# SSD mixer with y kept channels first, group roots through GpSimd's queue, and the convolutions dealt out one per weight piece

## The chip, the cores and the metric

The kernel runs on one core of one Trainium2 chip. The metric is the device time of the whole program in microseconds. TensorE is called PE here, its weight loads PEld, VectorE DVE, ScalarE ACT, GpSimd POOL, SyncE SP.

## The reference

A two-layer decoder trunk over 256 tokens of width 2048. Layer 0 is a Mamba-2 mixer, layer 1 an attention over keys and values made from layer 0's output. The change lies in layer 0, which computes, cut to what matters:

```
def _ssd_mixer(h, in_w, conv_w, conv_b, dt_bias, A_log, D_skip, norm_g, out_w):
    z, xBC, dt = jnp.split(h @ in_w, [4096, 4096 + 6144], axis=-1)
    xBC = jax.nn.silu(_causal_depthwise_conv(xBC, conv_w, conv_b))
    xs, Bm, Cm = jnp.split(xBC, [4096, 5120], axis=-1)        # 64 heads of 64; 8 groups of 128
    dt = jax.nn.softplus(dt + dt_bias); A = -jnp.exp(A_log)
    y = _ssd_chunked(xs * dt[..., None], dt * A, Bm, Cm)      # one chunk of 256 tokens
    y = y + (xs * D_skip[:, None]).reshape(bsz, L, 4096)
    y = y * jax.nn.silu(z)
    yg = y.reshape(bsz, L, 8, 512)
    yg = yg * lax.rsqrt(jnp.mean(jnp.square(yg), -1, keepdims=True) + RMS_EPS)
    return (yg.reshape(bsz, L, 4096) * norm_g) @ out_w
```

With one chunk and no state before it, y of a group is (C B^T, times the decays of its eight heads, causal) times the dt-scaled x. All is float32. A product with a weight is made of three matmuls: a value a is split into a high half that the fast form holds exactly and the low rest, and hi·hi, hi·lo and lo·hi are summed.

## The kernel before

**Weights.** Every weight comes in pieces of 128 x 1024 floats (512 KB), loaded by `load_piece` through SP's queue into `raw` (six buffers). `split` (lines 97 to 103) makes the halves: ACT copies the high half `whi` (line 100), DVE subtracts to the low half `wlo` (line 102); there are four buffers of each.

**Two forms of product.** In `cm_piece` (lines 141 to 153) the weight stands in the array and the activations move, 256 columns (all tokens) at a time; the output has channels on partitions. A piece is 24 matmuls. In `tm_piece` (lines 213 to 235) the activations stand and the weight moves, 512 columns at a time; the output has tokens on partitions. A piece is 12 matmuls. `cm_quad` and `tm_chunk` run the pieces of one output of 512 channels; `cm_wide` is a third form for 256 channels with both halves of the activations moving together.

**Order.** The opening (to about 175 us) makes h from the condition vector column by column on DVE (line 317) and already runs pieces of several products, in an order written out by hand (lines 540 to 552); partial sums are put away in tiles that are free by then (`begun`, lines 378 to 381). In that order stand 27 pieces of z products. Then a loop over the eight groups of the SSD follows (lines 835 to 849). In one round: the B and C product (every second round), the scores of group g, the x product of group g+1, the root scaling of group g-1 (`stage3`), the decays of group g and its x turned to tokens first (`stage1`), the four convolutions of group g+1 one after the other, the z product of group g+1, the head products of group g (`stage2`). The last z product carries group 7's scores and the first y tiles (`last_product`).

z, and with it y, have tokens on partitions: `stage2` multiplies the masked scores (standing, 64 columns at a time) with 64 channels, the sum of squares comes out of ACT's square (`accum_out`, line 812), the root scales rows on ACT (`stage3`), and `y_tiles` (lines 857 to 869) turns y back to channels first by 64 transposes on PE, scales it by the norm weight and splits it into halves for the out projection.

**Out projection.** Four chunks of 512 outputs with 16 pieces each (lines 942 to 965). Chunk 0 turns the y of one more group before every second piece (`y_ahead`). `background` takes jobs from a list at a fixed rate: these are the remaining columns of the condition product, each 1 MB from HBM and one DVE instruction of 128 x 2048 (line 317), and `gate_out`, which turns the finished gate into a row, writes it to HBM, and from there it is broadcast.

**What sets the order on an engine.** The text above is traced, and a planner orders each engine's queue when the whole program is traced, by the order of the text among what it reckons to be ready; `tc.issue_after` pins one instruction behind another. Each engine's queue, SP's and POOL's DMA queues too, then runs in that order. POOL does nothing before the last 15 us.

## Time and profile before

| | |
|---|---|
| median of three runs | 1224.19 us (1223.19 to 1224.21) |
| the profiled execution | 1223.81 us, its span 1222.0 |
| granted clock | 0.999 |
| PE, DVE, ACT, POOL busy | 99%, 83%, 58%, 0% |
| HBM read | 331.45 MB, 274 GB/s over the span |

A line of a group reads: line, engine, operation, output and inputs, shapes, count, then busy time and mean duration, then the idle time of the engine before them and what ended it. Records of matmuls overlap, so their mean duration is longer than the distance between them; the pace is read from start times. A line of the timeline or the chain begins with its start and length in us.

### The profile page before, as it was taken

Reading aid. Unit: us, or ns where it says so; the run is one execution under the profiler, and the core shown is the slowest. Engines: PE = TensorE matmul, PEld = TensorE weight load, DVE = VectorE, ACT = ScalarE, POOL = GpSimd, SP = SyncE. Lnnn points to the kernel's source line nnn. Section 1 sums busy time; section 2 is a strip of 40 time slices with the busy share of each in tenths; the row PEclk is TensorE's granted clock in tenths of the full one; section 3 lists DMA queues with packets and bytes.
Section 4 is the critical chain, followed back from the end, with each engine's and each line's share of the span. In section 5 each row is a group of like instructions: output and inputs, shape, how many; then the busy total and the mean of one; then the engine's idle time right before and its main releaser. Section 6 shows DMA issues by size and latency. Waiting matters only on the chain.

```text
span 1222.0 us, 19072 instructions
## 1 busy us (share of the span) xinstructions
PE 1208.8 (99%) x7244; PEld 1039.5 (85%) x7244; DVE 1019.6 (83%) x1450; ACT 703.9 (58%) x1057; POOL 3.9 (0%) x8
## 2 busy tenths in 40 slices
PE   8999999999999999999999999999999999999998
PEld 8889998898888888788888888888888888888886
DVE  6989997899988999899778588888987885756886
ACT  4554567787698898764335455444435844444751
POOL 0000000000000000000000000000000000000001
PEclk9999999999999999999999999999999999999999
DMA  9999976796765556689998668989997875365673
GB/s 374 421 421 423 422 264 239 259 327 224 230 190 194 182 173 207 226 327 334 370 317 298 211 203 342 350 344 379 385 376 280 281 261 174 113 193 160 193 260 69
DMA packets 81372, 335.94 MB, mean 275 GB/s; under 512 B 9200, under 2 KB 9984, under 8 KB 68480
## 3 DMA queue, kind: packets, MB, share of 16 engines
q1 hardware_dynamic: 80496, 333.59, 75.6%
q0 software_dynamic: 576, 1.05, 0.6%
q8 instruction: 57, 0.93, 0.3%
q14 instruction: 35, 0.29, 0.1%
q10 hardware_dynamic: 208, 0.08, 0.0%
HBM read 331.45 MB, written 3.23 MB: 274 GB/s over the span
## 4 chain that ended last, share of the span: by engine, by line
PE 77%; DVE 13%; ACT 5%; DMA 3%; issue 2%; DVEq 0%; ACTq 0%
PE acc L224 25%; PE acc L190 21%; PE acc L193 11%; DVE wlo L102 4%; DVE araw L317 4%; PE acc L233 3%; PE acc L234 3%; PE acc L232 3%; DMA raw<-in_win 3%; ACT whi L100 2%; DVE cacc L391 2%; PE acc L151 1%; PE acc L153 1%; PE acc L152 1%; PE py L809 1%
## 5 line engine op out<-in xcount | busy, mean ns | idle before, releaser
L100 ACT ACTIVATE whi<-raw 128x1024 fp32r<-128x1024 f32 x389 | 408.2, 1057 | 329.5 <-PE acc L190 107.1
L102 DVE TENSOR_TENSOR wlo<-raw,whi 128x1024 fp32r<-128x1024 f32 x389 | 470.2, 1221 | 128.3 <-ACT whi L100 121.1
L190 PE MATMUL acc<-actT,whi 128*128 128x512 f32 x1280 | 401.7, 394 | 0.5 <-DVE xs L202 0.5
L193 PEld LDWEIGHTS acc<-actT,wlo 128*128 128x128 f32 x1280 | 239.6, 188 | 52.3 <-DVE wlo L102 0.7
L193 PE MATMUL acc<-actT,wlo 128*128 128x256 f32 x1280 | 255.2, 281 | 0.3 <-DVE wlo L102 0.3
L317 DVE SCALAR_TENSOR_TENSOR araw<-araw,cb__72 128x2048 f32<-128x2048 f32 x95 | 217.0, 2284 | 3.2 <-DMA araw<-in_ada 3.0
L190 PEld LDWEIGHTS acc<-actT,whi 128*128 128x128 f32 x1280 | 195.0, 188 | 1.7 <-DVE xs L202 0.9
L224 PE MATMUL acc<-whi,actT 128*128 128x512 f32 x560 | 144.5, 392 | 0.5 <-ACT whi L100 0.5
L224 PEld LDWEIGHTS acc<-whi,actT 128*128 128x128 f32 x560 | 104.2, 188 | 22.0 <-ACT whi L100 0.9
L233 PE MATMUL acc<-wlo,actT 128*128 128x512 f32 x272 | 106.8, 393 | 2.2 <-DVE wlo L102 2.1
L232 PE MATMUL acc<-whi,actT 128*128 128x512 f32 x272 | 105.0, 394 | 0.2 <-ACT sz L664 0.2
L151 PE MATMUL acc<-actT,whi 128*128 128x256 f32 x372 | 103.5, 281 | 1.0 <-ACT sz L664 0.5
L224 PE MATMUL acc<-wlo,actT 128*128 128x512 f32 x384 | 103.6, 391 | 0.0
L153 PE MATMUL acc<-actT,wlo 128*128 128x256 f32 x372 | 101.9, 281 | 1.5 <-DVE wlo L102 1.5
L152 PE MATMUL acc<-actT,whi 128*128 128x256 f32 x372 | 103.0, 279 | 0.0
L234 PE MATMUL acc<-whi,actT 128*128 128x512 f32 x256 | 100.0, 391 | 0.0
L224 PEld LDWEIGHTS acc<-wlo,actT 128*128 128x128 f32 x384 | 71.7, 188 | 14.4
L151 PEld LDWEIGHTS acc<-actT,whi 128*128 128x128 f32 x372 | 69.6, 188 | 2.6 <-ACT sz L664 0.9
L153 PEld LDWEIGHTS acc<-actT,wlo 128*128 128x128 f32 x372 | 68.9, 188 | 2.3 <-DVE wlo L102 2.3
L152 PEld LDWEIGHTS acc<-actT,whi 128*128 128x128 f32 x372 | 70.6, 190 | 0.2
L233 PEld LDWEIGHTS acc<-wlo,actT 128*128 128x128 f32 x272 | 51.1, 188 | 13.8 <-DVE wlo L102 3.7
L232 PEld LDWEIGHTS acc<-whi,actT 128*128 128x128 f32 x272 | 50.9, 188 | 10.5 <-ACT sz L664 0.6
(324 smaller groups left out, 1293.5 us busy)
## 6 DMA issues: line engine op xcount, KB each, us to landing
araw<-in_ada SPq DMA_DIRECT2D x96, 1024.0 KB, 7.3
raw<-in_win SPq DMA_DIRECT2D x109, 512.0 KB, 6.0
raw<-in_wout SPq DMA_DIRECT2D x64, 512.0 KB, 5.7
raw<-in_wbin SPq DMA_DIRECT2D x64, 512.0 KB, 4.1
raw<-in_wxs SPq DMA_DIRECT2D x48, 512.0 KB, 4.5
raw<-in_wv SPq DMA_DIRECT2D x48, 512.0 KB, 6.7
raw<-in_wk SPq DMA_DIRECT2D x48, 512.0 KB, 7.6
cbc<-cumd SPq DMA_DIRECT2D x16, 512.0 KB, 5.1
```

What stands on the lines that cost most here:

```text
L100: copied.append(S.activation(hi, raw, AF.Copy))
L102: latest.append(V.tensor_tensor(lo, raw, hi.bitcast(F32), op=ALU.subtract))
L151: T.matmul(o, hi[:, k, c_], ahi[:, kt, :], start=first, stop=False, skip_group_check=True)
L152: T.matmul(o, hi[:, k, c_], alo[:, kt, :], start=False, stop=False, skip_group_check=True)
L153: T.matmul(o, lo[:, k, c_], ahi[:, kt, :], start=False, stop=kt == k1 - 1, skip_group_check=True)
L190: T.matmul(ps[n], hi[:, k, n * P:n * P + P], both(kt), start=kt == 0, stop=False, skip_group_check=True)
L193: T.matmul(ps[n][:, 0, :], lo[:, k, n * P:n * P + P], high(kt), start=False, stop=kt == KT - 1, skip_group_check=True)
L224: T.matmul(ps[b], a_(kt)[:, b * P:b * P + P], w_[:, k, :], start=a_ is ahi and w_ is hi and kt == k0, stop=w_ is lo and kt == k1 - 1)
L232: T.matmul(o, h_, hi[:, k, :], start=kt == k0, stop=False, skip_group_check=part)
L233: T.matmul(o, h_, lo[:, k, :], start=False, stop=False, skip_group_check=part)
L234: end = T.matmul(o, l_, hi[:, k, :], start=False, stop=kt == k1 - 1, skip_group_check=part)
L317: return V.scalar_tensor_tensor(raw, raw, 1.0, cb_, op0=ALU.mult, op1=ALU.mult, accum_out=mod[layer][:, ct, j:j + 1])
```

## The change

What changes, part by part:

- z is computed with `cm_quad`, so with channels on partitions, in the opening and in the loop; `tm_chunk` serves only the out projection and layer 1.
- y of a group is a tile of 128 x 4 x 256 (channels in four tiles, tokens along the row). The head products have x (64 channels) standing and 128 tokens of masked scores moving; the state product is four matmuls of 128 columns. The decay factors of the second half of the tokens are exponentials of the broadcast sums (`grow`), made on ACT. The D term is four scaled copies on ACT in place of two DVE multiplications.
- The sum of squares goes over partitions: one square on ACT into z's tile, two sums on DVE, two matmuls of one column against ones. The root goes to HBM (`rootd`) through POOL's DMA queue and comes back as a broadcast to all partitions, again through POOL: singly for groups 0, 1, 6 and 7, in one for groups 2 to 5. DVE scales y by norm weight and root in one step per channel tile (`y_scale`), and `y_split` makes the halves: one instruction of 1024 columns on ACT and one on DVE.
- The four convolutions of an x group become `chores`: one is taken after each weight piece of the following products; what is left is done before the next `stage1`, and in round 6 at once.
- In the out projection chunks 0 and 1 run their first 14 pieces each, then the last two of chunk 0 and of chunk 1, which hold group 7. Group 7's sums and root are traced in front of piece 1 of chunk 0, its tiles in front of piece 2 of chunk 1. Background jobs come once in three pieces there (before: one in two in chunk 0 and one in four later), then two in five.
- The second stage's matmuls are pinned behind the last product in groups 0, 2, 3, 4 and 7 (before: 0, 4 and 7), and one behind another.

The diff, cut:

```diff
-    def cm_quad(src, ahi, alo, rate=(0, 1), k0=0):
+    def cm_quad(src, ahi, alo, rate=(0, 1), k0=0, pre=None):
         ps = acc_pair()
         for q in range(k0 // 2, KT // 2):
+            if pre:
+                pre(q)
...
             background(*rate)
+            if chores:
+                chores.pop(0)()
+        z_end[:] = [end]
         return ps
...
+                return [lambda n=n: conv(t[:, n, :], 4 * g + n, t[:, n, :]) for n in range(4)]
...
+                ps = cm_quad(src, hhi, hlo, rate=R, k0=k0, pre=pre)
                 if kind == "z":
-                    ps = tm_chunk(src, hh_, hl_, rate=R, k0=k0, pre=pre, low_last=False)
...
+                    for n, rows_ in enumerate((slice(0, 64), slice(64, 128))):
+                        S.activation(grow[rows_, 2 * w:2 * w + 2, :], cbc[rows_, n:4:2, 1, :], AF.Exp)
...
+                for i in range(4):
+                    S.activation(y[g][:, i, :], xs[g][:, i, :], AF.Copy, scale=pv("dsk")[:, 4 * g + i:4 * g + i + 1])
+                return segs, xd, cb, xo, grow
...
+                behind = z_end[-1] if g in (0,2,3,4,7) else None
+                for i in range(4):
+                    c_ = slice(i * P, i * P + P)
+                    with tc.issue_after(behind.ins) if behind is not None else ExitStack():
+                        behind = T.matmul(po[:, c_], xo[:, c_], cb[:, 2, :], start=True, stop=True)
+                xo = xo.rearrange("p (i n) -> p i n", i=4)
+                V.tensor_tensor(xo, po.rearrange("p (i n) -> p i n", i=4), grow, op=ALU.mult)
+                V.tensor_tensor(y[g][:, :, P:], xo, y[g][:, :, P:], op=ALU.add)
+                for w in range(2):
+                    py = aux2.tile([P, 2, L], F32, name="py")
+                    for b in range(2):
+                        for hh in range(4):
+                            h = 4 * w + hh
+                            t_ = slice(64 * (hh % 2), 64 * (hh % 2) + 64)
+                            with tc.issue_after(behind.ins):
+                                behind = T.matmul(py[t_, hh // 2, b * P:b * P + P], xd[:, b, 64 * h:64 * h + 64],
+                                         segs[w][:, hh, b, :], start=True, stop=True)
+                    c_ = slice(2 * w, 2 * w + 2)
+                    V.tensor_tensor(y[g][:, c_, :], py, y[g][:, c_, :], op=ALU.add)
+                V.tensor_tensor(y[g], y[g], sz[g], op=ALU.mult)
+                sq = sz[g]
+                S.activation(sq, y[g], AF.Square)
+                return sq
+
+            def stage3(g, sq):
+
+                V.tensor_tensor(sq[:, 0:2, :], sq[:, 0:2, :], sq[:, 2:4, :], op=ALU.add)
+                sums = sq[:, 0, :]
+                V.tensor_tensor(sums, sums, sq[:, 1, :], op=ALU.add)
+                ss = (aux if g == G - 1 else aux2).tile([P, 512], F32, name="aux" if g == G - 1 else "py")[:, :2]
                 for b in range(2):
+                    T.matmul(ss[:, b:b + 1], sums[:, b * P:b * P + P], ones[:, 0:1], start=True, stop=True)
                 ms = sm.tile([P, 2], F32, name="ms")
                 V.tensor_scalar(ms, ss, 1.0 / 512, EPS, op0=ALU.mult, op1=ALU.add)
+                nc.gpsimd.dma_start(rootd[g * L:g * L + L].rearrange("(b p) -> p b", p=P), rsqrt(ms, "a"))
...
-                convolve = product("xs", g + 1)
+                convs = product("xs", g + 1)
+                while chores:
+                    chores.pop(0)()
                 if rs is not None:
                     stage3(g - 1, rs)
                 st1 = stage1(g, cb)
-                convolve()
+                chores.extend(convs)
+                while chores and g == G - 2:
+                    chores.pop(0)()
...
+            def y_scale(g):
+
+                if g < 2:
+                    roots[g] = p0.tile([P, L], F32, name="cacc", bufs=3)
+                    bcast(roots[g], rootd, g * L, queue=PO)
+                elif g in (2, 6):
+                    t = slots.tile([P, 4, L], F32, name=f"s{g // 6}")
+                    roots.update({g + j: t[:, j, :] for j in range(min(4, G - g))})
+                    n = min(4, G - 1 - g)
+                    bcast(t[:, :n, :].rearrange("p i l -> p (i l)"), rootd, g * L, queue=PO)
+                elif g == G - 1:
+                    bcast(roots[g], rootd, g * L, queue=PO)
+                for i in range(4):
+                    V.scalar_tensor_tensor(y[g][:, i, :], y[g][:, i, :], pv("normg")[:, 4 * g + i:4 * g + i + 1],
+                                           roots[g], op0=ALU.mult, op1=ALU.mult)
+
+            def y_split(g):
+
+                val = y[g].rearrange("p i (j r) -> p i r j", r=2)
+                hi, lo = (t.rearrange("p i (r j) -> p i r j", r=2) for t in y_to(g))
+                S.activation(hi, val, AF.Copy)
+                V.tensor_tensor(lo, val, hi.bitcast(F32), op=ALU.subtract)
...
         def y_ahead(q):
+            if q == 1:
+                with tc.high_priority():
+                    stage3(G - 1, rs)
+            if q % 2 == 0 and q // 2 + 1 < G - 1:
                 y_tiles(q // 2 + 1)
...
+        def out_pieces(n, q0, q1, pre=None):
+            for q in range(q0, q1):
+                if pre:
+                    pre(q)
+                tm_piece(wout[n], q, pss[n], out_of(0), out_of(1), 0, 2 * KT, low_last=True)
+                background(1, 3)
+
+        out_pieces(0, 0, KT - 2, y_ahead)
+        out_pieces(1, 0, KT - 2, lambda q: y_tiles(G - 1) if q == 2 else None)
+        drain()
...
+        for n in range(2):
+            out_pieces(n, KT - 2, KT)
+            joined(n, pss[n])
+        for n in range(2, 4):
+            ps = tm_chunk(wout[n], out_of(0), out_of(1), nk=2 * KT, rate=(2, 5), pre={3: first_weights}.get(n),
+                          split_end=4 if n == 3 else 0)
```

168 lines of the change are left out of this document (63 added, 105 removed).

## The prediction

> **What bounds the kernel now.** I read the page first, then the windows by stage, the waits, the pace of matmuls in the timeline, and last the two places where VectorE (DVE) sets the pace.
>
> ```profile
> span 1222.0 us, 19072 instructions
> PE 1208.8 (99%) x7244; PEld 1039.5 (85%) x7244; DVE 1019.6 (83%) x1450; ACT 703.9 (58%) x1057; POOL 3.9 (0%) x8
> PE 77%; DVE 13%; ACT 5%; DMA 3%; issue 2%; DVEq 0%; ACTq 0%
> ```
>
> The profiled run took 1223.81 us, 1.8 more than its span, and 0.4 less than the median of the three timed runs (1224.19). PE is busy for 99%, but overlapped records hide a PE that is paced by others. So the windows and the waits:
>
> ```profile
> 126.00:142.00 16.00, 16.00 (x134) 15.81 (x133) 15.44 (x18) 5.58 (x7) 0.00 (x0) 1.00 1.02 422
> 454.00:482.00 28.00, 28.00 (x253) 24.35 (x250) 26.44 (x50) 24.97 (x48) 0.00 (x0) 1.00 0.65 214
> 482.00:511.00 29.00, 28.30 (x196) 22.88 (x192) 25.57 (x50) 23.10 (x43) 0.00 (x0) 1.00 0.47 164
> 511.00:562.00 51.00, 51.00 (x252) 41.46 (x252) 49.40 (x77) 30.47 (x50) 0.00 (x0) 1.00 0.85 314
> PE acc L233 <- DVE wlo L102: 2.1, 3, 1.0
> ```
>
> The columns are stretch, length, busy time of PE, PEld, DVE, ACT and POOL, granted clock, DMA share, GB/s. PE is full in the opening (first row), in the SSD loop (454 to 482) and at the start of the out projection (511 to 562), while DVE stands at 94 to 97% beside it in all three. Only the last z product (482 to 511) leaves DVE 3.4 us. PE's longest wait in all is 2.1 us, on the low half of a weight. So the time is PE's queue: a matmul taken away is gained, one added is lost, and DVE has next to nothing to spare where the change gives it work.
>
> The pace of the two forms of product:
>
> ```profile
> 561.67 119.72 PE acc L224 x528
> 143.00 0.28 PE L152 MATMUL acc<-actT,whi 128*128 128x256 f32 x1
> 143.47 0.28 PE L153 MATMUL acc<-actT,wlo 128*128 128x256 f32 x1
> 210.11 0.28 PE L152 MATMUL acc<-actT,whi 128*128 128x256 f32 x1
> 211.92 0.28 PE L153 MATMUL acc<-actT,wlo 128*128 128x256 f32 x1
> ```
>
> A matmul of 512 columns takes 119.72/528 = 0.2267 us, a piece of 12 then 2.72 us. Of 256 columns, the five matmuls from 143.00 to 143.47 (in the opening) stand 0.1175 us apart, the seventeen from 210.11 to 211.92 (a bc product of the loop) 0.113.
>
> **1. The y transposes go (-8.2).** With y kept channels first, the 64 transposes of y_tiles vanish.
>
> ```profile
> L864 PE MATMUL aux<-cc,s 128*128 128x128 f32 x64 | 11.8, 274 | 0.0
> 510.83 0.66 PE L864 MATMUL aux<-cc,s 128*128 128x128 f32 x4
> 511.25 2.09 PE L224 MATMUL acc<-whi,xs 128*128 128x512 f32 x8
> 530.03 0.38 PE L864 MATMUL aux<-cc,s 128*128 128x128 f32 x2
> 530.16 0.48 PE L224 MATMUL acc<-whi,actT 128*128 128x512 f32 x1
> 530.48 0.38 PE L864 MATMUL aux<-cc,s 128*128 128x128 f32 x2
> ```
>
> Four in a row hold PE for 0.42 us (510.83 to 511.25). A pair costs 0.13, and the matmul behind it 0.32 in place of 0.227: coming back to the weights costs 0.09 each time. Over the whole chunk n=0, from 511.25 to 561.67, 16 pieces of 2.72 would be 43.5 us and 50.4 passed, so the transposes in it were worth 6.9. The eight of group 0 in the last z product add 2 x 0.42 + 4 x 0.09 = 1.2, and a bit over. I take 8.2; bounds 7.5 and 9.
>
> **2. The state and head matmuls (-1.4), and the sums (+2.8).**
>
> ```profile
> 240.75 1.02 PE L798 MATMUL aux<-xo,cb 128*128 128x512 f32 x2
> 241.70 2.08 PE L809 MATMUL py<-xd,seg 128*64 128x64 f32 x64
> 243.71 0.38 PE L151 MATMUL acc<-actT,whi 128*128 128x256 f32 x1
> ```
>
> The head products take 2.01 us per group now: 64 instructions of 64 columns, 0.031 each, since the two halves of the array run side by side (a lone 128-column one takes 0.105, above; 64 would take half). Afterwards they are 32 of 128 columns, again alternating halves: 32 x 0.105/2 + some 0.15 = 1.83, so -0.18 per group, -1.4 for eight. Were the halves not side by side, it would be 32 x 0.105 = 3.4, +11 in all: the far bound. The state product (0.95) becomes four products of 128 columns, eight instructions of 0.105: even. New are two matmuls of one column per group (four instructions) that sum the squares over partitions. No row shows one column; between 0.031 (64 columns) and 0.105 (128 with a full weight), nearer the middle as the weight is full, 4 x 0.065 + 0.09 for coming back = 0.35, times 8 = +2.8; bounds 1.7 and 4.1.
>
> **3. z turned round (+2.8).** All 64 z pieces go from 12 matmuls of 512 to 24 of 256. In the order of the opening stand 27 z pieces, 37 follow in the loop. In the loop 24 x 0.113 = 2.72, even. In the opening the nearest row is 0.1175 for the same form in the same stretch: 27 x 24 x 0.0042 = +2.7, with rounding 2.8. If the slower pace belongs to those products and not to the stretch, it is 0: bounds 0 and 2.8. What could hide it is a wait of PE there, and the first window has none. A rule to weigh: the Trainium skill (TensorE: Matmul & The Clock Gate, "Back-to-back issue gap") gives a warm gap of columns over the clock plus about 2.5 ns for each matmul. By it the 768 added matmuls cost an estimated 1.9 us anywhere; the loop's 0.113 against half of 0.2267 shows no such cost, the opening shows more, so I keep the rows.
>
> **4. Start of the out projection (+2.2).** DVE sets the pace there already:
>
> ```profile
> 515.84 0.16 DVE L814 TENSOR_SCALAR ms<-ss 128x2 f32<-128x2 f32 x1
> 525.26 0.15 DVE L281 SCALAR_TENSOR_TENSOR ay<-at,ay 128x2 f32<-128x2 f32 x1
> 544.45 2.28 DVE L317 SCALAR_TENSOR_TENSOR araw<-araw,cb__72 128x2048 f32<-128x2048 f32 x1
> 546.66 0.87 DVE L869 SCALAR_TENSOR_TENSOR ylo<-aux,prm,actT 128x256 fp32r<-128x256 f32 x2
> 547.45 2.35 DVE L102 TENSOR_TENSOR wlo<-raw,whi 128x1024 fp32r<-128x1024 f32 x2
> 550.84 2.28 DVE L317 SCALAR_TENSOR_TENSOR araw<-araw,cb__72 128x2048 f32<-128x2048 f32 x1
> ```
>
> A round of two pieces lasts 6.39 us (544.45 to 550.84): two weight splits 2.27, a gate column 2.21, four L869 at 0.40. Afterwards PE wants 2 x 2.72 = 5.44 per round. DVE has two splits 2.27, four scalings by root and norm weight 1.6 (like L869), one low half of 1024 columns 1.14 (like a split), and at one column in three pieces 1.47: 6.48. Five rounds (groups 2 to 6) are 5.2 short; the first round carries group 7's tail (about 5.5: state multiply and add, two head adds, the gate multiply, two sums, the root) and comes out 4.9 short. Against that stand three pieces split ahead (3.4) and PE's own 3.0 on group 7's matmuls: 3.7 short, of which the fourth column (2.2) may trail: 1.5 to 3.7, I take 2.2. The idle 3.4 before 511 is no help: the scalings of groups 0 and 1 and the low half of group 0 (3.2 + 1.1 for 1.6 now) take 2.7 of it. Lower bound 0: group 7's tail is wanted only 28 pieces later and may run behind the rest. The second chunk stands beside it with DVE work of 1.14 + 0.74 per piece, so nothing builds up. Group 7, moved behind 28 pieces, is off the path: 76 us cover its chain. The gate row must now arrive within about five pieces (13.6 us) of its column:
>
> ```profile
> s<-gated SPq DMA_DIRECT2D x3, 256.0 KB, 8.6
> gated<-row SPq DMA_DIRECT2D x2, 8.0 KB, 2.5
> out<-u POOLq DMA_DIRECT2D x4, 256.0 KB, 8.1
> cbc<-cumd SPq DMA_DIRECT2D x16, 512.0 KB, 5.1
> ```
>
> 2.5 + 8.6 + about 1 for the transpose and copy is 12.1: hidden by 1.5; without that cover the third chunk starts late by as much as the rest, up to 3 us if loads ahead on SP hold it.
>
> **5. The loop (-1.5).** The largest PE wait there follows a burst:
>
> ```profile
> 228.72 2.76 DVE cacc L391 x7
> 231.47 1.14 DVE wlo L102
> 232.66 0.50 PE acc L233
> ```
>
> Seven convolution steps run before the split that PE stands for. One convolution behind each weight piece breaks such runs; of the 2.1 us I take 1.5. DVE per group: the two multiplications by D go (0.68 each), two sums of 512 and 256 columns come (0.68 + 0.42), so -0.3.
>
> ```profile
> L781 DVE TENSOR_TENSOR s<-aux,prm 128x512 f32<-128x512 f32 x16 | 10.9, 680 | 0.0
> L820 ACT ACTIVATE s<-s,ay 128x512 f32<-128x512 f32 x16 | 10.9, 715 | 2.0 <-DVE ay L281 2.0
> L868 ACT ACTIVATE actT<-aux,prm 128x256 fp32r<-128x256 f32 x28 | 12.3, 468 | 9.0 <-PE aux L864 9.0
> ```
>
> ACT per group loses two copies (1.4) and wins four multiplications by D and four exponentials of 256 columns, like L868 at about 0.4: 3.2. That is +1.8, less 0.3 for one square in place of two. In 454 to 482 it idles 3.0, so it lies beside. Bounds -2.1 to +4 (ACT late).
>
> **Sum:** -8.2 - 1.4 + 2.8 + 2.8 + 2.2 - 1.5 = -3.3 on 1223.8: 1220.5, on the scale of the median **1220.9**.
>
> **Rivals.**
> *More gain:* DVE keeps up at 511 (group 7's tail runs late) and the opening costs nothing: -3.3 - 2.2 - 2.8 = -8.3, 1215.9. For it: loop pace 0.113. Against: DVE's 97%.
> *Roots late (the slow side):* POOL's queue holds the write of group 7's root and the broadcast of roots 2 to 5, traced in that order. If they run so, the broadcast waits for the root, now ready at 525.4, 14.2 after the chunk's start, later by the sums (1.3); write and broadcast then take 1.3 + 6.6 (between the 5.1 of SP's broadcast and POOL's 8.1): 23.4, and 2.7 of scaling and split follow, where piece 4 wants group 2 at 10.9. PE stands about 15: -3.3 + 15 = +11.7, 1235.9; half of it when only the landing is slow, 1229. It decides once roots 2 to 5 land over 8.2 after the chunk's start. Against: the broadcast needs only slot s0 and old roots, and DVE's row shows the queues filled by readiness, not by the order of the text (the root's steps from 515.84 to 525.26 with other work between). The Trainium skill (SBUF — State Buffer, "SBUF: two separate sides") says that a GpSimd DMA's descriptors starve while DVE holds the port the two share; that would lengthen this landing, and no run here shows it.
> *ACT paces the loop:* one more pair of table loads per group besides its +1.5 uses up the 3.0: about 1 per group in four groups and no smoothing: -3.3 + 1.5 + 4 = +2.2, 1226.4.
> *Halves not side by side:* +11 + 1.4 - 3.3 = +9, 1233. Against: 0.031 per instruction today.
> That the convolutions still run in one burst, since the planner orders by readiness, is -1.8, inside the forecast.
>
> **How the numbers follow.** Forecast 0.44, own range 1218 to 1224; more gain 0.24; ACT 0.13; roots 0.14; halves 0.05. About 0.2% (2.4 us, below 1221.7 or above 1226.6) is what a measurement of this kernel can tell from no change. The forecast puts 0.30 below and 0.14 within; more gain is faster; ACT 0.10 within and 0.03 above; roots 0.01 within and 0.13 above; halves above. Faster 0.54, same 0.25, slower 0.21. The range 1214 to 1231 takes in more gain (down to its cheapest sums, 1.1 less, and transposes at 9), ACT, and roots half late; fully late roots and the halves stay out.
>
> **What would show it.** Chunk n=0 and n=1 together near 32 x 2.72 + 2.2 = 89 us (step 4), with PE waits on DVE's low halves, not on a root's DMA; the head products near 1.83 us per group; one-column matmuls near 0.065; z pieces in the opening at 0.1175 per matmul (step 3) and in the loop at 0.113; no wait over 1 us behind a run of convolutions. A DVE wait on the roots' tile, or ACT near 100% in the loop, makes the prediction wrong.

## The result and the profile after

The changed kernel took **1242.39 us** (median of four runs, 1239.67 to 1243.53) against 1223.98 for the kernel before on the same chip: ratio 1.0145, 95% interval 1.0129 to 1.0161. It is slower by 18 us where 3 were forecast as a gain, and it lies outside the range. The profiled execution took 1239.67 us with a span of 1237.9, 15.9 more than the span before.

The page's first lines and its chain of waits:

```profile
span 1237.9 us, 20135 instructions
PE 1210.2 (98%) x7772; PEld 1074.4 (87%) x7772; DVE 1026.0 (83%) x1450; ACT 718.2 (58%) x1060; POOL 12.4 (1%) x21
PE 67%; DVE 14%; ACT 9%; DMA 6%; issue 3%; SPq 0%; ACTq 0%; DVEq 0%
```

PE's share of the chain fell from 77% to 67%, and ACT's rose from 5% to 9%. The windows by stage (columns as before) show where PE now stands:

```profile
216.00:233.00 17.00, 14.14 (x123) 13.93 (x123) 12.19 (x19) 15.01 (x27) 0.00 (x0) 1.00 0.56 216
454.00:482.00 28.00, 28.00 (x205) 25.43 (x204) 25.15 (x50) 26.43 (x48) 0.72 (x1) 1.00 0.51 179
496.00:523.00 27.00, 24.57 (x187) 23.40 (x188) 25.07 (x49) 17.24 (x27) 1.26 (x2) 0.94 0.69 124
523.00:540.00 17.00, 12.05 (x70) 9.65 (x67) 16.14 (x27) 10.20 (x11) 0.55 (x1) 0.90 0.84 321
```

The stretch from which the prediction read ACT's room (454 to 482) is still full on PE. The time is lost in groups 0 and 2 of the loop, in the last z product and at the start of the out projection, and in the last two the granted clock is below 1 too.

**The loop.** PE's, ACT's and DVE's rows of the timeline around the first large wait (start, us, engine, line, operation, tiles, count; idle time before and its releaser in brackets):

```profile
229.04 0.28 PE L152 MATMUL acc<-actT,whi 128*128 128x256 f32 x1
232.18 0.38 PE L153 MATMUL acc<-actT,wlo 128*128 128x256 f32 x1 [2.86 <-DVE wlo L102]
216.68 1.04 ACT L100 ACTIVATE whi<-raw 128x1024 fp32r<-128x1024 f32 x1
217.63 1.05 ACT L759 ACTIVATE seg<-seg 128x1024 f32<-128x1024 f32 x1
218.70 0.42 ACT L761 ACTIVATE grow<-cbc 64x256 f32<-64x256 f32 x1
219.14 2.45 ACT L757 ACTIVATE seg<-cbc,cumT 128x128 f32<-128x128 f32 x8
221.50 0.40 ACT L761 ACTIVATE grow<-cbc 64x256 f32<-64x256 f32 x1
221.81 1.04 ACT L759 ACTIVATE seg<-seg 128x1024 f32<-128x1024 f32 x1
222.88 0.41 ACT L761 ACTIVATE grow<-cbc 64x256 f32<-64x256 f32 x1
223.31 2.96 ACT L100 ACTIVATE whi<-raw 128x1024 fp32r<-128x1024 f32 x3
217.76 1.22 DVE L102 TENSOR_TENSOR wlo<-raw,whi 128x1024 fp32r<-128x1024 f32 x1 [1.74 <-ACT whi L100]
222.88 1.22 DVE L762 TENSOR_TENSOR seg<-seg,cb 128x1024 f32<-128x1024 f32 x1 [2.77 <-ACT seg L759]
224.41 1.23 DVE L102 TENSOR_TENSOR wlo<-raw,whi 128x1024 fp32r<-128x1024 f32 x1 [0.30 <-ACT whi L100]
228.54 2.44 DVE L396 SCALAR_TENSOR_TENSOR cacc<-xs,prm,cacc 128x255 f32<-128x255 f32 x6
```

ACT and DVE in the kernel before:

```profile
216.96 1.04 ACT L100 ACTIVATE whi<-raw 128x1024 fp32r<-128x1024 f32 x1
217.90 2.15 ACT L765 ACTIVATE seg<-cbc,cumT 128x128 f32<-128x128 f32 x7
219.96 1.05 ACT L100 ACTIVATE whi<-raw 128x1024 fp32r<-128x1024 f32 x1
220.91 1.05 ACT L767 ACTIVATE seg<-seg 128x1024 f32<-128x1024 f32 x1
221.85 1.99 ACT L100 ACTIVATE whi<-raw 128x1024 fp32r<-128x1024 f32 x2
218.23 1.22 DVE L102 TENSOR_TENSOR wlo<-raw,whi 128x1024 fp32r<-128x1024 f32 x1
221.03 1.22 DVE L102 TENSOR_TENSOR wlo<-raw,whi 128x1024 fp32r<-128x1024 f32 x1 [1.59 <-ACT whi L100]
223.31 1.22 DVE L102 TENSOR_TENSOR wlo<-raw,whi 128x1024 fp32r<-128x1024 f32 x1
```

Between 216.7 and 223.8 us ACT makes four high halves of weights in the kernel before and one in the changed kernel: the growth factors, and the decay steps bunched between them, take the places of the splits. DVE stands 2.77 us for the second decay tile (`seg`) and so writes two low halves (`wlo`) from 217 to 225 us, where it wrote three. Behind that it has the same run of other work in both kernels, about 5 to 7 us long, up to the next low half at 230.90 (before: 231.40); it ends with convolution steps, still six in a row although the program text deals them out (before: seven). With one low half less in hand PE now runs dry for 2.86 us where it waited 0.98 before. SP's queue is no part of this: in 205 to 345 us it stood 5.3 us until the growth factors had been read from the broadcast tile `cbc`, but 13.0 us for the same tile in the kernel before.

**The start of the out projection.** PE, then DVE:

```profile
522.65 1.97 PE L802 MATMUL py<-seg,xd 128*64 128x128 f32 x32
524.55 1.20 PE L232 MATMUL acc<-wlo,xs 128*128 128x512 f32 x4
528.33 1.09 PE L232 MATMUL acc<-whi,actT 128*128 128x512 f32 x4
532.99 0.58 PE L818 MATMUL aux<-cc,sz 128*128 128x1 f32 x4 [3.57 <-DVE sz L815]
534.95 2.07 PE L232 MATMUL acc<-whi,ylo 128*128 128x512 f32 x4 [1.38 <-DVE ylo L885]
531.43 0.69 DVE L813 TENSOR_TENSOR sz<-sz 128x512 f32<-128x512 f32 x1
532.43 0.42 DVE L815 TENSOR_TENSOR sz<-sz 128x256 f32<-128x256 f32 x1
533.61 0.16 DVE L820 TENSOR_SCALAR ms<-aux 128x2 f32<-128x2 f32 x1 [0.36 <-PE aux L818]
533.68 1.21 DVE L885 TENSOR_TENSOR ylo<-s,actT 128x1024 fp32r<-128x1024 f32 x1
```

PE has used up group 0's pieces at 529 and needs group 1's low half. DVE writes it only at 533.68, straight after group 7's sums, and those sums also stand in PE's queue ahead of the piece.

**An account of PE.** For each pair of successive matmuls I took the time from start to start beyond that form's own pace. An excess over 0.15 us is a wait; matmuls that follow each other at about twice the time are slow pace. Waits and slow pace add to 11.1 us in the whole trace before and 34.4 after; smaller excess goes from 15.8 to 14.0. That is 21.5 more, the span grew by 15.9, so the matmuls' own time fell by 5.6. In the table below "loop" is 205 to 495 us and "out" 495 to 700 us, waits and slow pace together, each from the one profiled execution; the times are medians of all runs.

| kernel | loop | out | time, us | ratio to before, 95% |
|---|---|---|---|---|
| before | 3.2 | 1.5 | 1224.0 | |
| changed | 10.7 | 11.8 | 1242.4 | 1.0145 (1.0129 to 1.0161) |
| changed, other session (e17) | 13.7 | 13.8 | 1246.1 | 1.0177 (1.0160 to 1.0194) |
| e1 convolutions at once | 10.9 | 11.9 | 1240.1 | 1.0123 (1.0108 to 1.0138) |
| e2 D on DVE | 7.4 | 13.8 | 1236.6 | 1.0089 (1.0071 to 1.0107) |
| e3 growth once | 6.4 | 11.7 | 1236.6 | 1.0095 (1.0080 to 1.0110) |
| e4 squares of 7 moved | 12.1 | 11.4 | 1240.4 | 1.0127 (1.0109 to 1.0146) |
| e5 e2 and e3 | 6.4 | 12.6 | 1237.3 | 1.0109 (1.0093 to 1.0125) |
| e6 low half, own space | 14.6 | 15.4 | 1247.1 | 1.0186 (1.0171 to 1.0201) |
| e7 all three | 5.7 | 17.4 | 1237.4 | 1.0113 (1.0090 to 1.0136) |
| e8 all three, burst | 7.7 | 16.3 | 1240.6 | 1.0133 (1.0116 to 1.0150) |
| e9 Silu before pieces | 3.1 | 10.8 | 1232.2 | 1.0065 (1.0050 to 1.0080) |
| e10 gate later | 5.9 | 17.2 | 1238.2 | 1.0101 (1.0076 to 1.0126) |
| e11 own space, gate later | 3.4 | 22.4 | 1245.9 | 1.0171 (1.0156 to 1.0186) |
| e12 no scalings | 14.2 | 15.6 | 1246.2 | 1.0176 (1.0160 to 1.0191) |
| e13 roots of 7 later | 5.9 | 8.6 | 1230.3 | 1.0044 (1.0028 to 1.0059) |
| e14 low half first | 3.6 | 7.9 | 1229.0 | 1.0036 (1.0023 to 1.0049) |
| e15 start alone | 17.6 | 12.6 | 1246.1 | 1.0171 (1.0154 to 1.0188) |
| e16 loop alone | 3.4 | 12.7 | 1233.7 | 1.0078 (1.0057 to 1.0099) |
| e18 before, ACT loaded | 8.1 | 8.5 | 1235.5 | 1.0088 (1.0072 to 1.0104) |

The loop's column falls into two sets. The seven executions with the changed kernel's work on ACT (the two of the changed kernel, e1, e4, e6, e12 and e15) have 10.7 to 17.6; the eleven with less of it (e2, e3, e5, e7 to e11, e13, e14 and e16) have 3.1 to 7.7. Within the first set the loop's work is nearly the same, so several us of it differ from one execution to the next without an edit.

### The profile page after: what moved, and what is told of

Its sections match the earlier page's. It is cut to its first block, busy times and chain, and to the rows that moved or that the text cites. A ratio compares the mean times of both kernels' runs of the same rounds, so it can differ in the third digit from the quotient of the medians.

```text
span 1237.9 us, 20135 instructions
## 1 busy us (share of the span) xinstructions
PE 1210.2 (98%) x7772; PEld 1074.4 (87%) x7772; DVE 1026.0 (83%) x1450; ACT 718.2 (58%) x1060; POOL 12.4 (1%) x21
## 4 chain that ended last, share of the span: by engine, by line
PE 67%; DVE 14%; ACT 9%; DMA 6%; issue 3%; SPq 0%; ACTq 0%; DVEq 0%
PE acc L232 23%; PE acc L196 19%; PE acc L199 10%; DVE wlo L102 4%; DMA raw<-in_win 4%; DVE araw L324 3%; ACT whi L100 3%; PE acc L153 3%; PE acc L151 2%; PE acc L152 2%; DVE cacc L396 2%; ACT seg L757 1%; PE acc L242 1%; PE acc L240 1%; PE acc L241 1%
## 5 line engine op out<-in xcount | busy, mean ns | idle before, releaser
L199 PEld LDWEIGHTS acc<-actT,wlo 128*128 128x128 f32 x1280 | 239.5, 188 | 55.0 <-DVE wlo L102 2.7
L199 PE MATMUL acc<-actT,wlo 128*128 128x256 f32 x1280 | 254.8, 280 | 1.8 <-DVE wlo L102 1.8
L153 PE MATMUL acc<-actT,wlo 128*128 128x256 f32 x884 | 242.7, 280 | 10.0 <-DVE wlo L102 9.8
L151 PE MATMUL acc<-actT,whi 128*128 128x256 f32 x884 | 245.8, 280 | 0.6 <-ACT sz L661 0.4
L152 PE MATMUL acc<-actT,whi 128*128 128x256 f32 x884 | 244.6, 278 | 0.0
L196 PEld LDWEIGHTS acc<-actT,whi 128*128 128x128 f32 x1280 | 194.7, 188 | 0.6
L153 PEld LDWEIGHTS acc<-actT,wlo 128*128 128x128 f32 x884 | 165.4, 190 | 12.2 <-DVE wlo L102 12.0
L151 PEld LDWEIGHTS acc<-actT,whi 128*128 128x128 f32 x884 | 167.2, 189 | 2.2 <-ACT sz L661 0.6
L152 PEld LDWEIGHTS acc<-actT,whi 128*128 128x128 f32 x884 | 167.4, 189 | 0.2 <-issue 0.2
L232 PE MATMUL acc<-whi,actT 128*128 128x512 f32 x560 | 143.6, 391 | 0.5 <-ACT whi L100 0.5
L232 PEld LDWEIGHTS acc<-whi,actT 128*128 128x128 f32 x560 | 104.5, 188 | 22.8 <-ACT whi L100 0.9
L232 PE MATMUL acc<-wlo,actT 128*128 128x512 f32 x384 | 103.7, 392 | 0.0
L232 PEld LDWEIGHTS acc<-wlo,actT 128*128 128x128 f32 x384 | 72.6, 189 | 16.0
L232 PE MATMUL acc<-whi,ylo 128*128 128x512 f32 x208 | 57.4, 398 | 1.4 <-DVE ylo L885 1.4
L757 ACT ACTIVATE seg<-cbc,cumT 128x128 f32<-128x128 f32 x128 | 40.7, 388 | 2.5 <-DMA cbc<-cumd 1.7
```

The costliest lines, as they stand in the source:

```text
L151: T.matmul(o, hi[:, k, c_], ahi[:, kt, :], start=first, stop=False, skip_group_check=True)
L152: T.matmul(o, hi[:, k, c_], alo[:, kt, :], start=False, stop=False, skip_group_check=True)
L153: end = T.matmul(o, lo[:, k, c_], ahi[:, kt, :], start=False, stop=kt == k1 - 1, skip_group_check=True)
L196: T.matmul(ps[n], hi[:, k, n * P:n * P + P], both(kt), start=kt == 0, stop=False, skip_group_check=True)
L199: T.matmul(ps[n][:, 0, :], lo[:, k, n * P:n * P + P], high(kt), start=False, stop=kt == KT - 1, skip_group_check=True)
L232: T.matmul(ps[b], a_(kt)[:, b * P:b * P + P], w_[:, k, :], start=a_ is ahi and w_ is hi and kt == k0, stop=w_ is lo and kt == k1 - 1)
```

## The experiments

My theory after the result had two parts: in the loop, ACT's new work stands ahead of the weights' high halves; at the start of the out projection, group 1's low half waits for the space that group 7's squares hold. The rivals were the dealt-out convolutions, DVE's load, and roots that come late. An edit also lets the planner order the queues anew (in e18 PE takes group 1's scores at 228 us, in the kernel before at 260), so what a run shows is the edit together with its new order.

### e1 to e4: one part each

e1 undoes the dealing out:

```
-                while chores and g == G - 2:
+                while chores:
```

> The four x convolutions of a group run at once behind stage1 again; all else is as in the changed kernel. Theory (ScalarE's new work, the growth factors and the multiplications by D, stands ahead of the weights' high halves, and the squares of group 7 hold the space of the low halves): dealing the convolutions out is not the cause, so 1240 to 1244 us, with the waits of TensorE on low halves near 229 and 320 us still there. Rival (the dealt-out convolutions, one behind each weight piece, delay the weight splits): 1232 to 1237 us and those waits gone.

1240.1 us, the waits of the loop as before it (10.9 against 10.7): dealing out is not the cause. The 2 us are within what the changed kernel itself moves between sessions (e17).

e2 adds x by D on DVE for groups 0 to 6:

```
-  V.tensor_tensor(y[g][:, c_, :], py, y[g][:, c_, :], op=ALU.add)
+  for i in (2 * w, 2 * w + 1):
+      V.scalar_tensor_tensor(y[g][:, i, :], xs[g][:, i, :], D_i, py[:, i % 2, :], op0=ALU.mult, op1=ALU.add)
```

> The multiplication of x by D leaves ScalarE for groups 0 to 6: VectorE takes it in the addition of the head products (four fused steps of 256 columns in place of two additions of 512). Theory (ScalarE ahead of the weights' high halves): 1.7 us per group less on ScalarE, TensorE's waits near 229 and 320 us shrink from 3.0 to under 1.5, 4 to 8 us gained, 1234 to 1238. Rival (VectorE is the bound, ScalarE lies beside): no gain or up to 2 us slower, 1242 to 1244.

1236.6 us (1233.4 to 1240.7): the time is as the theory said, though DVE got more to do, and 3.5 below e1 and e4 of the same session. Of the two waits only the one near 320 us went; the one of group 0 stayed (3.47 us up to 234.62), with the growth factors still on ACT there.

e3 computes the growth factors for group 0 alone:

```
-  for n, rows_ in enumerate((slice(0, 64), slice(64, 128))):
+  for n, rows_ in enumerate((slice(0, 64), slice(64, 128)) if not g else ()):
```

> The growth factors are computed for group 0 alone and every group multiplies by those (the other groups' exponentials are left out, so the output differs). It takes 1.7 us per group off ScalarE and nothing off VectorE or TensorE. Theory (ScalarE ahead of the weights' high halves): 4 to 8 us gained, 1234 to 1238. Rival (VectorE or the order of the convolutions): within 1 us of the changed kernel, 1241 to 1243.

1236.6 us, again 3.5 below e1 and e4. The wait near 320 us went; the one near 229, in group 0 whose factors are still computed, stayed at 2.9.

e4 moves group 7's squares:

```
-  sq = sz[g]                        (for group 7)
+  sq7 = slots.tile([P, 4, L], F32, name="s1"), squared after y_tiles(1)
```

> The squares of group 7 are written into the slot of group 1's y, free once group 1 is split, and no longer into group 7's z tile. Theory (the low halves of y lie in space that is free only when the z tile's last reader is done; since the squares stay in it, that reader is TensorE's sum at 533 us): group 1's low half is written at about 526 in place of 533.7, TensorE's gap of 528 to 535 closes to under 1.5 us, and with the half clock behind it 6 to 8 us are gained: 1234 to 1236.5. Rival (VectorE is full there with the scalings and group 7's tail, the space is free in time): 0 to 2 us gained.

1240.4 us. DVE in e4:

```profile
529.47 1.22 DVE L102 TENSOR_TENSOR wlo<-raw,whi 128x1024 fp32r<-128x1024 f32 x1 [0.50 <-ACT whi L100]
530.61 3.49 DVE L887 TENSOR_TENSOR ylo<-s,actT 128x1024 fp32r<-128x1024 f32 x3
```

The low half came 3.1 us earlier and no longer stands behind the sums. So the squares do hold its space. But it came at 530.6 and not at 526: it now stands behind group 7's multiplication by z (527.7), then the last reader of the z tile in the program text. PE's idle time from 529 us on shrank from 4.9 us (3.57 and 1.38) to 2.3, and a new wait of 1.9 came before 581: the time hardly moved, as the rival said.

### e5 to e8: together

e5 is e2 and e3 in one:

> Both earlier edits together: x by D added on VectorE for groups 0 to 6, and the growth factors of group 0 used for all groups (the other groups' exponentials are left out, so the output differs). ScalarE then has less to do per group than in the kernel before. Theory (in the loop ScalarE stands ahead of the weights' high halves; the two edits took 3.0 and 4.2 us off TensorE's waits between 205 and 345 us, which were 7.2): those waits come down to the 2.3 of the kernel before, the heads of group 2 stand at 338 to 340 us, and the time is 1232 to 1235, no lower since the waits of 495 to 540 us stay near 10. Rival (the two edits remove the same waits, and others stay): no better than one of them alone, 1236 to 1238.

1237.3 us: no better than one alone, as the rival said. The wait near 229 us (2.8) was still there, since group 0 still computed its factors.

e6 gives group 1's low half its own space:

```
+  ylo[1] = slots.tile([P, 4, L], F32R, name="s0")
-  roots of groups 2 to 5 in slot s0, ahead
+  root of group 2 alone ahead, those of 3 to 6 in the space given back
+  squares of group 7 in slot s1, as in e4
```

> ScalarE's work is as in the changed kernel. Group 1's low half is written into group 0's slot, which is free before the last z product ends, and not into space given back by the tiles of the groups; group 2's roots come alone into a small tile ahead of the last z product's end, those of 3 to 6 later; group 7's squares go into group 1's slot as in the last run on this. Theory (TensorE's gap of 528 to 535 us comes from the order that the space forces: the low half stood behind group 7's multiplication by z at 527.7 and, through it, behind six scalings): the low half is written by 527, the waits of 495 to 540 us fall from 8.8 to 3 or 4, and 5 to 8 us are gained without a new wait behind: 1234 to 1237. Rival (VectorE has more to do there than TensorE needs time, wherever the pieces stand): the wait comes back later, as at 579 us, and the gain is 2 us or less, 1240 to 1242.

1247.1 us: the theory of the start fell in this form, no gain at all. Its 5 us over the first timing of the changed kernel are 0.9 over the second (e17).

e7 puts the loop's two edits and e6 together, the growth factors now by one small exponential and a broadcast:

```
+  S.activation(growr, cumr[:, P:], AF.Exp); nc.sync.dma_start(growd, growr)
+  PO.dma_start(grow[rows_], growd of heads 8 g + n, + 2, + 4, + 6)
```

> The three together, and the whole computation: the exponentials of the growth factors are taken once for all heads in one small step (64 rows of 128) and fetched per group by a broadcast on GpSimd's queue; x by D is added on VectorE for groups 0 to 6; group 1's low half has its own space. Theory (three separate causes that add up): 5.8 for each of the first two less the overlap, and 5 to 8 for the start: 1225 to 1230, with TensorE's waits of 205 to 345 us at 2 to 3 and of 495 to 540 at 3 to 4. If the matrix work saved (5.6 us) came out whole, 1219 would be the floor. Rival (what is taken away at one place comes back at the next, since VectorE stands at 93 to 97%): 1232 or more.

1237.4 us, the rival's side: loop 5.7, out 17.4. DVE idled 8.3 us (514.7 to 523.0, for a weight's high half) and was full from 530 to 560: the scalings that used to run ahead in such idle time now could not.

e8 is e7 with the convolutions at once:

> As the run of all three, with the four x convolutions of each group at once behind stage1, as in the kernel before. Theory (dealing them out is worth little either way once ScalarE is light): within 2 us of the run of all three. Rival (a burst of convolutions holds the low halves back): 3 us or more slower, with a wait of TensorE of over 1 us behind seven or more steps of the convolutions in the loop.

1240.6 us, 3.2 more than e7. But e7's runs spread over 6.5 us, and e8 has 2.0 more in the loop and 1.1 less in "out": that dealing out gains something once ACT is light is not shown.

### e9 to e12: order or load

e9 is e7 with the low half back at its place in the changed kernel, group 7's squares where e4 has them, and two splits issued behind group 1's high half:

```
+  with tc.issue_after(his[1].ins) if n == 0 and q in (2, 3) else ExitStack():
+      w = split(load_piece(wout[n][q]))
```

> As the run of all three, but group 1's low half lies where the changed kernel puts it, with group 7's squares in group 1's slot; and the splits of the out projection's third and fourth weight piece are issued only behind group 1's high half, so that on ScalarE the last Silu and that half no longer stand behind a split that waits for a buffer from TensorE (9.3 us from 512.6 to 521.9 in the run of all three). The scalings of groups 2 to 4 run ahead again, in VectorE's idle time. Theory (the start of the out projection is lost to the order on ScalarE's and VectorE's queues): TensorE's waits of 495 to 540 us fall from 8.4 to 4 or 5 and those of 540 to 700 from 6.0 to under 3, 1228 to 1232. Rival (VectorE has too much work there in sum): the waits only move, 1235 to 1238.

1232.2 us, at the edge of the theory's range. The loop has no more waits than before the change (3.1), and those from 495 to 540 us came down to 4.5; those behind stayed at 6.3, where under 3 was forecast. What was left in e9 showed on DVE:

```profile
561.17 1.67 DVE L892 SCALAR_TENSOR_TENSOR s<-s,prm,s 128x256 f32<-128x256 f32 x4 [5.08 <-DMA s<-rootd]
```

Here the roots are late indeed: DVE's queue stood 5.08 us for group 7's, and PE 2.4 us for the weight split behind it.

e10 is e9 with the gate columns begun after 11 pieces:

```
-  background(1, 3)
+  background(1, 2), from state[0] = -9
```

> As the run before this one, and the eight gate columns of the out projection begin after 11 pieces in place of 3, then one in two pieces: some two or three columns of 2.3 us leave VectorE's queue in the first 30 us. Theory (order alone): no change within 1 us against that run. Rival (VectorE's load at the start): 3 to 6 us faster than it, 1225 to 1228, with TensorE's waits of 540 to 700 us under 1.

1238.2 us, 6 slower. Taking load off DVE's first 30 us gave nothing here, but the run can't decide about load: the columns, now closer together, were late themselves, and behind them a weight piece (ACT stood 7.08 us for one at 562.24):

```profile
561.35 2.29 DVE L324 SCALAR_TENSOR_TENSOR araw<-araw,cb__72 128x2048 f32<-128x2048 f32 x1 [9.95 <-DMA araw<-in_ada]
```

e11 joins the same with e6's space:

> As the run of all three (group 1's low half in its own space, scalings of groups 3 to 6 behind it), with ScalarE's order mended and the gate columns begun after 11 pieces. Theory (order alone): VectorE idled 8.3 us ahead of the last z product's end in the run of all three since the scalings could not run ahead, and that stays, so the waits behind 520 us stay at 8 or more and it is 2 to 4 us slower than the two kernels above. Rival (load at the start): with the columns gone VectorE keeps up and it is as fast as or faster than them.

1245.9 us: the space of its own costs, in the place where the theory put it and by more than it said.

e12 leaves out scalings in the changed kernel:

```
-  for i in range(4):
+  for i in range(4 if g < 2 else 0):
```

> The changed kernel, without the multiplication of y by its roots and norm weights for groups 2 to 7 (left out, so the output differs): 9.6 us less on VectorE between 510 and 560 us, of which six steps or 2.4 us stand ahead of group 1's low half. Theory (group 1's low half waits for group 7's sums to free its space): the sums come 2.4 us earlier, so 2 to 4 us gained, and a TensorE gap of 3 us or more stays ahead of the first use of that half. Rival (VectorE's load alone): the gap closes, 6 to 9 us gained, 1233 to 1236.

1246.2 us, the same as the changed kernel in e17, though DVE had 9.6 us less to do. The PE wait at the sums stayed (4.2 us). Both forecasts of a gain were wrong, so the load of the scalings alone is not the cause. DVE even stood 6.2 us up to 530 us for a weight's high half, which itself had waited 7.2 us for its transfer, with the last Silu behind it.

### e13 to e16: what is left, and each half alone

e13 is e9 with group 7's scaling issued at the ninth piece of the second chunk in place of the third:

```
-  lambda q: y_tiles(G - 1) if q == 2 else None
+  lambda q: y_tiles(G - 1) if q == 8 else None
```

> The kernel of 1232.2 us (ScalarE light, Silu and group 1's high half ahead of the third and fourth piece's split), with group 7's scaling and split issued at the ninth piece of the second chunk in place of the third. Theory (in that kernel VectorE's queue stood 5.1 us for the broadcast of group 7's roots, and the weight split behind it cost TensorE 2.4 us and 1.8 of half clock at 561 us): those waits go, 3.5 to 4.5 us gained, 1227.5 to 1229. Rival (the pieces' transfers are late there anyway, ScalarE waited 4.1 us for one): under 1 us gained.

1230.3 us. DVE no longer waits for the roots, and the waits of "out" fell from 10.8 to 8.6. The 1.9 us below e9 are half of the forecast, and as e9 ran in another session they are too few to be read as a gain (e17).

e14 is e13 with those two splits' low halves issued behind group 1's low half too:

```
+  w = split(load_piece(wout[n][q]), after=los[1].ins if n == 0 and q in (2, 3) else None)
```

> As the run before this one, and the low halves of the out projection's third and fourth weight piece are computed behind group 1's low half. Theory (TensorE stands 2.0 us at 519 for group 1's low half, 1.1 of it for that split): 1 us gained against the run before, 1226.5 to 1228. Rival (the split is then what TensorE waits for): no gain.

1229.0 us, the best version with the change, and still 0.36% above the kernel before. It is 1.3 below e13, but the two kernels' runs overlap. PE in e14 waits twice more for weight splits, 1.1 and 1.6 us.

e15 is the start's edits of e9 on the changed kernel:

> The changed kernel with the start's edits alone: group 7's squares in group 1's slot, and the splits of the third and fourth piece behind group 1's high half. ScalarE's work in the loop is as in the changed kernel. Theory (two causes that add up): the loop's waits stay at 7 or more, those of 495 to 540 us fall from 8.8 to 5 or 6, 3 to 5 us gained, 1237 to 1239.5. Rival (all of it comes from ScalarE's load, the start only follows): 0 to 1.5 us gained.

1246.1 us, as the changed kernel in e17: in time the rival's forecast. But PE's waits of 495 to 540 us fell to 5.5, as the theory said (8.8 in the changed kernel); new ones of 2.65 and 1.44 us came behind (at 580 and 677), and the loop's 17.6 were the highest of all. So the waits at the start moved, and the time says little of what the edits are worth.

e16 is the loop's edits of e7 on the changed kernel:

> The changed kernel with the loop's edits alone: the growth factors from one small exponential for all heads and a broadcast, x by D on VectorE for groups 0 to 6; the start as in the changed kernel. Theory (two causes that add up): TensorE's waits of 205 to 345 us at 1.5 to 2.5, those of 495 to 540 still 8 or more, 6 to 8 us gained, 1234.5 to 1236.5. Rival (the loop's gain is lost again at the start, since TensorE then reaches it earlier than VectorE): 1238 or more.

1233.7 us, the largest single gain, and 12.4 below e15 of the same session. Group 7's scores stand at 488.9 us, against 496.4 in the changed kernel and 487.9 before. ACT in e16, where the high halves come early again (DVE then writes three low halves from 217 to 225 us, as before the change), and then PE at its start:

```profile
216.53 1.04 ACT L100 ACTIVATE whi<-raw 128x1024 fp32r<-128x1024 f32 x1
219.52 1.05 ACT L100 ACTIVATE whi<-raw 128x1024 fp32r<-128x1024 f32 x1
221.42 1.99 ACT L100 ACTIVATE whi<-raw 128x1024 fp32r<-128x1024 f32 x2
518.38 1.09 PE L232 MATMUL acc<-whi,actT 128*128 128x512 f32 x4
524.90 0.99 PE L831 MATMUL aux<-cc,sz 128*128 128x1 f32 x4 [5.43 <-DVE sz L828]
527.27 1.22 PE L232 MATMUL acc<-whi,ylo 128*128 128x512 f32 x2 [1.38 <-DVE ylo L898]
```

The start's gap is there unshortened, with ACT light and PE in time. So it is a loss of its own.

### e17 and e18: the changed kernel again, and ACT's load in the kernel before

> The changed kernel again, as it was. Theory (the three kernels with ScalarE's load and other starts lost 4 us to the start's new order or to the loop's): 1240 to 1244 us as at first. Rival (they are no slower than the changed kernel; the loop's waits near 229 and 322 us differ from session to session): 1244.5 to 1247.

e17 took 1246.1 us, 3.8 more than at first and as its rival said, while the kernel before stayed within 0.8 (1224.0 and 1224.7). So differences of up to 4 us between sessions are not to be read as effects of an edit; the times of e1, e4, e6, e12 and e15 show none.

e18 adds ACT's new work to the kernel before, results unused:

```
+  S.activation(grow[rows_, 2 * w:2 * w + 2, :], cbc[rows_, n:4:2, 1, :], AF.Exp)
+  S.activation(grow (256 columns), xs[g][:, i, :], AF.Copy, scale=D_i)          (four)
```

> The kernel before, with the new work of ScalarE added and its results unused: four exponentials of the growth factors and four multiplications of x by D per group, 3.4 us (the output stays the same). TensorE's and VectorE's work is that of the kernel before. Theory (ScalarE's new work stands ahead of the weights' high halves): 4 to 8 us slower than before, 1228 to 1232, TensorE's waits of 205 to 345 us up from 2.3 to 5 or more, the first near 229 us. Rival (ScalarE has the room, 3.0 us idle in 28, and the loop's loss comes from the other forms of the matrix work or from VectorE's): 0 to 1.5 us slower.

1235.5 us against 1224.7: 10.8 slower, with no other part of the change. DVE and PE in e18:

```profile
222.67 1.23 DVE L770 TENSOR_TENSOR seg<-seg,cb 128x1024 f32<-128x1024 f32 x1 [2.76 <-ACT seg L767]
232.02 0.50 PE L233 MATMUL acc<-wlo,actT 128*128 128x512 f32 x1 [2.90 <-DVE wlo L102]
```

The same two waits, at the same place and of the same length as in the changed kernel. The loop's sum (8.1) was smaller than forecast between 205 and 345 us and larger behind. Group 7's scores stand at 493.6 us, 5.7 later than before the change; the other half of the loss comes behind them, where PE waits four times from 496 to 504 us (3.7 us in all) and the granted clock is 0.77 from 495 to 510. As a price of ACT's new work in the changed kernel the 10.8 may be too high: here nothing is taken off ACT, while the change takes away the scalings by the root (10.9 us in all) and half of the squares' instructions, though not at this place.

## Why the prediction was wrong

**Steps 1 and 2 were right.** The transposes are gone, and nothing came in their place on PE. The head products of a group take 1.90 us (522.65 to 524.55 above), forecast 1.83. The one-column sums and what follows them:

```profile
286.03 0.50 PE L818 MATMUL py<-cc,sz 128*128 128x1 f32 x4
286.39 1.07 PE L770 MATMUL aux<-cc,xs 128*128 128x128 f32 x8
```

0.36 us per group, forecast 0.35. The halves do run side by side.

**Step 3 was mis-sized, +2.8 for about 0.** The same form in the opening, after:

```profile
141.54 0.28 PE L152 MATMUL acc<-actT,whi 128*128 128x256 f32 x1
141.66 0.28 PE L153 MATMUL acc<-actT,wlo 128*128 128x256 f32 x1
141.77 0.28 PE L151 MATMUL acc<-actT,whi 128*128 128x256 f32 x1
```

0.115 us each, 0.113 as the most frequent value. The opening ends at 205.4 us where it ended at 205.2: by the account above waits grew from 2.2 to 4.9 and the small excess fell from 3.5 to 0.6. So the slower pace did not belong to the form, and the lower bound was the right end; what made the pace slower in the kernel before is not shown. Nor do the 2.5 ns per added matmul show that the step weighed: two of 256 columns take 0.226 us, one of 512 took 0.2267. With it the matmuls' own time was forecast at -8.2 - 1.4 + 2.8 = -6.8, and came out at -5.6 by the same account.

**Step 5 failed at "so it lies beside".** The term itself was nearly right: D costs 14.3 us over eight groups and the growth factors 13.2, which is 3.4 per group where 3.2 was forecast:

```profile
L781 ACT ACTIVATE s<-xs,prm 128x256 f32<-128x256 f32 x32 | 14.3, 500 | 0.2
L761 ACT ACTIVATE grow<-cbc 64x256 f32<-64x256 f32 x32 | 13.2, 413 | 0.5
```

The idle time of 3.0 us was read in 454 to 482, in one late group. What counts is where the work stands in ACT's queue: ahead of the second decay tile and the weights' high halves, for both of which DVE then stands. The sum of DVE's waits for high halves does not tell it (in 205 to 345 us 14.1 us in the changed kernel and 5.0 before, but 14.1 in e3 and 5.8 in e18 too); it is told by how many low halves are written ahead of DVE's next run of other work. The loop lost 8.5 us (487.9 to 496.4) for the -1.5 forecast; e16 gives 7.5 of it back, and e18 makes 5.7 of it in the kernel before. Nor was a gain of 1.5 to be had: the 2.1 us that the step took for one wait are the sum of three, and the one behind the burst of convolutions was 0.98. The rival *ACT paces the loop* named the engine, at 0.13 and with 5.5 us; it was worth more than that, and for the most part not by table loads: the lines of layer 0's SSD that have them show 27 against 23, at 1.28 us each 5.1 us in all, beside the 27.5 of the new steps.

**Step 4 failed at its +2.2, and in its reason.** It priced DVE's load and left group 7's tail free to run behind. Measured, the stretch from group 7's head products to the first transposes of x is 183.3 us before and after (508.8 to 692.1, 522.7 to 706.0), although eight of its matmuls (1.9 us) had already run: the 6.9 us of transposes were lost again there, and waits and slow pace up to 540 us grew by 10.8. e12 speaks against the load of the scalings as the reason, though a late transfer took its place there. The new squares stay in the z tile until PE has summed them, the low halves' space is free only then (e4: with the squares moved, the low half no longer stands behind the sums), and the sums stand ahead of the piece on PE. The prediction costed the sums as PE time and never asked what tile they hold. Before, the squares went to PSUM. Edits of the order recover a part: e16 to e14 gain 4.7 us. What costs the rest (7.9 in e14 against 1.5) stays open. One rival has no run of its own: from 495 to 545 us ACT stood 3.2 us for the transfer of a weight piece in the changed kernel, with the last Silu behind it (7.2 us in e12, 7.1 in five waits in e14), and for none in the kernel before.

**Roots late** did not happen in the changed kernel: no DVE wait on the roots' tile is in its trace, and POOL issued the broadcast of roots 2 to 5 at 511.49 us, ahead of the write of group 7's root (547.26). It is near, though: e9 shows it once.

## What to carry to other kernels

Room on an engine is to be read at the instruction that releases the bottleneck, in every repetition of the stage: 1.8 us more per group on ACT (718.2 us busy in all against 703.9), which had 3 us idle in one stretch, went with a loss of 8.5 us in the loop, since the new work came ahead of what PE waits for. Where an intermediate result moves to another tile, ask until when that tile is held now and who takes its space; the price is in the taker's queue. And work removed from the bottleneck is only gained where the next engine is not already in step with it: here the 6.9 us of transposes came back as waits.

## What the runs showed of the hardware

Half pace follows some waits of PE and not others of the same length. After 2.86 us at 229 us PE ran on at full pace; after 2.87 us at 320 us it ran at 0.21 us per matmul in place of 0.113 for 2.5 us, with a granted clock of 0.50 from 322.8 to 326.2:

```profile
323.26 0.58 PE L153 MATMUL acc<-actT,wlo 128*128 128x256 f32 x1 [2.87 <-DVE wlo L102]
323.65 0.41 PE L151 MATMUL acc<-actT,whi 128*128 128x256 f32 x1
323.86 0.41 PE L152 MATMUL acc<-actT,whi 128*128 128x256 f32 x1
```

The Trainium skill (TensorE: Matmul & The Clock Gate, "HAM oscillation — how this bites in real kernels") gives the rule of no idle gaps over some 3.4 us. Here a gap of 2.87 us was enough once, and one of 1.94 us in e13 (up to 268.62), while an equal one in e8 was not; so as a bound the rule is too lax for these traces. The changed kernel has three such stretches of 3.4 us at a granted clock of 0.50 ahead of its last microseconds (from 322.8, 507.1 and 534.4), the kernel before none.

Some kernels whose PE waits often also repeat worse: e2's runs spread over 7.4 us, e7's over 6.5, and the changed kernel's two medians lie 3.8 apart, where the kernel before's runs spread over 3.8 in all sessions, with medians within 0.7. It is no rule: e8's four runs lie within 0.4 us and e12's within 0.7.
